# More pairs of column blocks by seven products in the MLP, with their sums of weights on GpSimd

## The chip, the cores and the metric

The kernel runs on one core of one Trainium2 chip. The metric is the device time of one execution, in microseconds (us). A core has TensorE (PE) for products of matrices, VectorE (DVE), ScalarE (ACT) and GpSimd (POOL) for elementwise work, and SyncE (SP), whose queue issues nearly all loads here. All arithmetic is float32; a product runs as three products of a high and a low part.

## The reference, cut to what matters

Two layers, each with a block of four mixers and an MLP. Only the MLP is touched by the change:

```python
h2 = _rms(x, norm2_g[layer])
x = x + jnp.square(jax.nn.relu(h2 @ mlp_w1[layer])) @ mlp_w2[layer]
```

`x` is 256 by 2048, `mlp_w1` 2048 by 8192, `mlp_w2` 8192 by 2048.

## The kernel before

**Blocks and chunks.** W1 is cut into 16 blocks of 512 columns, W2 into 16 blocks as well (four rounds `rd` of 2048 rows by four blocks `n` of 512 columns). Each block is loaded in eight chunks of 512 KB (256 rows, held as 128 partitions by 1024). A chunk becomes a high part `wh` (a copy by ACT, line 154) and a low part `wl` (raw minus high part by DVE, line 155). `raw` has four buffers, `wh` three, `wl` two. `product_steps` then issues twelve matmuls of 512 columns for a chunk: two halves of it, two tiles of 128 rows of the left side, three products each (lines 181, 182, 186).

**Pairs by seven products.** For a pair of blocks (b, b+1) the 2 by 2 product of half chunks with half tiles of rows (two row tiles, two halves of 256 rows of weights) is made of seven products in place of eight. `first` makes two of them (p1, p2) from the plain chunks of block b: six matmuls a chunk. Then, chunk by chunk, `sums_prep` loads the chunk of block b again into `b1` and that of block b+1 into `b2`, makes four sums of weights of 128 by 512 (`t13` holds two, `t24` two; lines 256, 257, 260, 261, each from two tiles in SBUF), and splits them and half of `b2` into high and low parts (`bh`, `bl`, `t13h`, `t13l`, `t24h`, `t24l`; lines 248 and 249). `sums_step` issues 15 matmuls with them (p3 to p7). After eight chunks `combine` adds p1 to p7 to the four results c11, c12, c21, c22 and squares their positive parts. `b1` and `b2` have one buffer each, `t13` and `t24` alternate in two buffers of one tag, `t24h` and `t24l` have one each; `t13h` and `t13l` take buffers from the rings of `wh` and `wl`.

The sum chain of one chunk: t13's halves are b2's first half minus b1's first half, and b2's second half minus b2's first half; t24's first half is b2's second half minus t13's first half, and t24's second half is t24's first half minus b1's second half. So line 260 is the last sum that reads `b2`, and line 261 the last that reads `b1`.

**What sets the order.** `mlp` runs a plan: plain W1 products (`plain`) and W2 products (`second`), chunk by chunk. Each chunk advances a clock by 2.72; whenever the clock passes `due`, the generator `steps` is advanced by a step of the pairs and yields how much is added to `due` (2.4 a chunk of `first`, 2.1 each of the five steps of a chunk of sums). The result is then placed on the engines by a list scheduler when the program is built, so that each engine has one fixed order. `place` transposes finished columns into the left side of a later W2 round (four `slots` groups). Of W1's sixteen blocks eight are plain and eight go as four pairs in each layer; the plan is four plain products, then three W2 rounds with two plain products behind the first and the second, then the fourth round.

## Time and profile before

| what | us |
|---|---|
| median of three runs | 2246.22 (2244.64 to 2248.01) |
| the profiled execution, its own time | 2246.25 |
| its span on the core | 2244.5 |
| PE busy in the span | 2216.0 (99%) |
| DVE busy | 1629.5 (73%) |
| ACT busy | 1196.8 (53%) |
| POOL busy | 148.0 (7%) |

Busy time is the time in which at least one instruction of the engine was running; a matmul's end is modelled, so neighbouring matmuls overlap and their distance from start to start says what one costs. The first MLP lies at some 431 to 1102 us of the span, the second at some 1545 to 2240. The time is 1.75 us more than the span. 444.29 MB move by DMA, 198 GB/s over the span.

### The profile page before, as it was taken

How to read it: one execution, taken by the hardware profiler on the slowest of the kernel's cores; microseconds unless marked ns; L12 is line 12 of the kernel's file. 1: busy time of each engine (PE TensorE's matmuls, PEld its weight loads, DVE VectorE, ACT ScalarE, POOL GpSimd, SP SyncE). 2: the span in 40 equal slices, each digit the busy share in tenths (PEclk: the TensorE clock that was granted, in tenths of full speed). 3: DMA queues.
4: the chain of work that ended last, by engine and by line, in shares of the span. 5: the costliest groups of instructions: out<-in, count | busy, mean ns of one | idle time of the engine just before them, and what ended most of it. 6: DMA issues, size and time to landing. Idle time of an engine off the chain costs nothing.

```text
span 2244.5 us, 30247 instructions
## 1 busy us (share of the span) xinstructions
PE 2216.0 (99%) x10988; PEld 1814.2 (81%) x10988; DVE 1629.5 (73%) x2421; ACT 1196.8 (53%) x1588; POOL 148.0 (7%) x402
## 2 busy tenths in 40 slices
PE   8999999999999999999999999999999999999999
PEld 7788788888788787888888877888887888888887
DVE  8877666877777778776578766658777776777754
ACT  6465444765555645645545554447555555465443
POOL 1221220100000000000011321101000000000000
PEclk9999999999999999999999999999999999999999
DMA  7536445566765666656556363456666666666554
GB/s 254 164 115 200 154 141 196 184 227 209 237 219 210 226 214 225 227 198 209 181 185 187 100 234 123 155 193 204 221 213 233 214 218 231 219 226 218 184 197 169
DMA packets 125429, 444.29 MB, mean 198 GB/s; under 512 B 15072, under 2 KB 15328, under 8 KB 125280
## 3 DMA queue, kind: packets, MB, share of 16 engines
q1 hardware_dynamic: 122688, 439.67, 58.0%
q10 hardware_dynamic: 2592, 2.70, 0.4%
q8 instruction: 86, 1.41, 0.3%
q14 instruction: 63, 0.52, 0.1%
HBM read 440.21 MB, written 2.10 MB: 197 GB/s over the span
## 4 chain that ended last, share of the span: by engine, by line
PE 91%; DVE 3%; DMA 2%; POOL 2%; issue 1%; ACT 1%; DVEq 0%; SPq 0%; ACTq 0%
PE mm L186 24%; PE mm L181 23%; PE mm L182 23%; PE p L223 4%; PE p L225 4%; PE p L224 4%; PE tp L312 2%; DMA raw<-in_w_dram 1%; DVE wl L155 1%; PE yp L713 1%; PE bu L693 1%; PE glu L736 1%; PE nsc L944 0%; PE npv L954 0%; ACT wh L154 0%
## 5 line engine op out<-in xcount | busy, mean ns | idle before, releaser
L154 ACT ACTIVATE wh<-raw 128x1024 fp32r<-128x1024 f32 (+1 forms) x688 | 716.0, 1049 | 763.5 <-PE mm L182 548.9
L155 DVE TENSOR_TENSOR wl<-raw,wh 128x1024 fp32r<-128x1024 f32 (+1 forms) x688 | 830.9, 1212 | 295.6 <-PE mm L186 187.0
L181 PE MATMUL mm<-wh,Bl 128*128 128x512 f32 x1280 | 500.0, 391 | 2.0 <-ACT wh L154 2.0
L182 PE MATMUL mm<-wh,Bh 128*128 128x512 f32 x1280 | 500.6, 391 | 0.0
L181 PE MATMUL mm<-wh,Al 128*128 128x512 f32 (+1 forms) x1216 | 471.0, 389 | 4.5 <-ACT wh L154 4.5
L182 PE MATMUL mm<-wh,Ah 128*128 128x512 f32 (+1 forms) x1216 | 471.2, 389 | 0.0
L186 PE MATMUL mm<-wl,Bh 128*128 128x512 f32 x1280 | 350.1, 393 | 2.5 <-DVE wl L155 2.4
L186 PE MATMUL mm<-wl,Ah 128*128 128x512 f32 (+1 forms) x1216 | 333.6, 394 | 9.4 <-DVE wl L155 9.2
L181 PEld LDWEIGHTS mm<-wh,Bl 128*128 128x128 f32 x1280 | 240.3, 188 | 54.6 <-ACT wh L154 3.7
L186 PEld LDWEIGHTS mm<-wl,Bh 128*128 128x128 f32 x1280 | 237.9, 188 | 55.5 <-DVE wl L155 5.9
L182 PEld LDWEIGHTS mm<-wh,Bh 128*128 128x128 f32 x1280 | 240.3, 188 | 50.7
L186 PEld LDWEIGHTS mm<-wl,Ah 128*128 128x128 f32 x1216 | 222.6, 189 | 64.0 <-DVE wl L155 14.7
L181 PEld LDWEIGHTS mm<-wh,Al 128*128 128x128 f32 x1216 | 229.8, 189 | 53.2 <-ACT wh L154 5.3
L182 PEld LDWEIGHTS mm<-wh,Ah 128*128 128x128 f32 x1216 | 229.7, 189 | 46.8 <-issue 1.1
L249 DVE TENSOR_TENSOR t13l<-t,t13h 128x1024 fp32r<-128x1024 f32 x64 | 78.4, 1224 | 88.7 <-PE mm L186 68.8
L248 ACT ACTIVATE t13h<-t 128x1024 fp32r<-128x1024 f32 x64 | 67.8, 1059 | 108.4 <-PE mm L182 93.8
L1121 DVE TENSOR_TENSOR x<-mm,x 128x512 f32<-128x512 f32 x96 | 62.1, 685 | 54.3 <-PE mm L186 54.1
L249 DVE TENSOR_TENSOR t24l<-t,t24h 128x1024 fp32r<-128x1024 f32 x64 | 78.1, 1220 | 4.5 <-ACT t24h L248 4.5
L248 ACT ACTIVATE t24h<-t 128x1024 fp32r<-128x1024 f32 x64 | 67.0, 1047 | 1.3 <-DVE t L261 0.7
L326 DVE TENSOR_TENSOR Bl<-tp,Bh 128x512 fp32r<-128x512 f32 x76 | 51.1, 685 | 12.6 <-ACT Bh L325 12.4
L248 ACT ACTIVATE bh<-b 128x512 fp32r<-128x512 f32 x64 | 40.1, 627 | 30.9 <-DMA b<-in_w_dram 30.9
L325 ACT ACTIVATE Bh<-tp 128x512 fp32r<-128x512 f32 x76 | 43.3, 588 | 21.4 <-PE tp L312 20.8
(399 smaller groups left out, 2346.7 us busy)
## 6 DMA issues: line engine op xcount, KB each, us to landing
raw<-in_w_dram SPq DMA_DIRECT2D x448, 512.0 KB, 4.2
raw<-in_w_main_dram SPq DMA_DIRECT2D x160, 512.0 KB, 3.7
b<-in_w_dram SPq DMA_DIRECT2D x128, 512.0 KB, 4.1
raw<-in_w_out_dram SPq DMA_DIRECT2D x64, 512.0 KB, 3.8
aux<-in_wcmp_dram SPq DMA_DIRECT2D x16, 512.0 KB, 5.8
raw<-in_w_gate_dram SPq DMA_DIRECT2D x16, 268.0 KB, 2.8
x<-in_x_dram SPq DMA_DIRECT2D x8, 256.0 KB, 4.7
aux<-in_s5g_dram SPq DMA_DIRECT2D x4, 512.0 KB, 6.0
```

The lines of the kernel that those rows point to most:

```text
L154: self.nc.scalar.activation(h[:, :cols], r[:, :cols], AF.Copy)
L155: self.nc.vector.tensor_tensor(l[:, :cols], r[:, :cols], h[:, :cols].bitcast(F32), ALU.subtract)
L181: nc.tensor.matmul(acc[t], rows(xl, t), mov(wh, j), start=k == 0, stop=False)
L182: nc.tensor.matmul(acc[t], rows(xh, t), mov(wh, j), start=False, stop=False)
L186: nc.tensor.matmul(acc[t], rows(lhs[k][0], t), mov(wl, j), start=False, stop=k == nk - 1)
L223: nc.tensor.matmul(acc, xl, wh, start=first, stop=False)
L224: nc.tensor.matmul(acc, xh, wh, start=False, stop=False)
L225: nc.tensor.matmul(acc, xh, wl, start=False, stop=last)
L248: nc.scalar.activation(h, x, AF.Copy)
L249: V.tensor_tensor(l, x, h.bitcast(F32), ALU.subtract)
L326: nc.vector.tensor_tensor(l, pt, h.bitcast(F32), ALU.subtract)
L1121: self.nc.vector.tensor_tensor(x, acc[t], x, ALU.add)
```

## The change

In each layer seven pairs in place of four: only blocks 0 and 1 stay plain. The four sums of weights of a chunk move from DVE to GpSimd (`G`). A chunk of `first` now adds 1.05 to `due`, each step of a chunk of sums 0.84, and `due` starts at zero, so that pair 0 lies beside the two plain products and two pairs lie beside each of the first three W2 rounds; the fourth round has none. `combine` reads the products in another order, and results go to other buffers (`late`). Line numbers behind 244 grow by one: what was 256, 257, 260, 261 is 257, 258, 261, 262.

```diff
--- before.py
+++ after.py
@@ -241,6 +241,7 @@
 
         nc = self.nc
         V = nc.vector
+        G = nc.gpsimd
         f2 = lambda x: x.rearrange("p a b -> p (a b)")
         ahead = lambda: self.tc.high_priority(offset=self.prio - 100)
 
@@ -253,12 +254,12 @@
             nc.sync.dma_start(f2(b1), src1)
             nc.sync.dma_start(f2(b2), src2)
             ta, tb = (self.wk.tile([P, 2, 512], F32, name=nm, tag="aux", bufs=2) for nm in ("t13", "t24"))
-            V.tensor_tensor(ta[:, 0, :], b2[:, 0, :], b1[:, 0, :], ALU.subtract)
-            V.tensor_tensor(ta[:, 1, :], b2[:, 1, :], b2[:, 0, :], ALU.subtract)
+            G.tensor_tensor(ta[:, 0, :], b2[:, 0, :], b1[:, 0, :], ALU.subtract)
+            G.tensor_tensor(ta[:, 1, :], b2[:, 1, :], b2[:, 0, :], ALU.subtract)
         yield
         with ahead():
-            V.tensor_tensor(tb[:, 0, :], b2[:, 1, :], ta[:, 0, :], ALU.subtract)
-            V.tensor_tensor(tb[:, 1, :], tb[:, 0, :], b1[:, 1, :], ALU.subtract)
+            G.tensor_tensor(tb[:, 0, :], b2[:, 1, :], ta[:, 0, :], ALU.subtract)
+            G.tensor_tensor(tb[:, 1, :], tb[:, 0, :], b1[:, 1, :], ALU.subtract)
         yield
         with ahead():
             bh = self.wk.tile([P, 512], F32R, name="bh", tag="z")
@@ -279,7 +280,7 @@
     def sums_step(self, acc, w, slot, sums, first, last):
 
         if first:
-            for i in (3, 5, 7, 6, 4):
+            for i in (6, 3, 5, 7, 4):
                 pool, tag = (self.ps, "mm") if i == 4 else (self.pm, "ms")
                 acc[i] = pool.tile([P, 512], F32, name=f"p{i}", tag=tag)
         for i, m in ((3, 3), (5, 0), (7, 2), (6, 1)):
@@ -1166,11 +1167,13 @@
                     self.act2(hs[t], acc[t], r, t)
             at(now[0] + 5, lambda: place(rd, n, hs))
 
+        late = lambda i: i and i % 2 == 0
+
         def first(i, b):
             p = []
             yield from self.first_steps(p, w1(b), h2)
             with self.hp():
-                v, c = tmp("v", ("rtmp", "sq")[i % 2]), tmp("c11", "rp" if i % 2 else "ev")
+                v, c = tmp("v", ("rtmp", "sq")[i % 2]), tmp("c11", "rp" if late(i) else "ev")
                 nc.scalar.activation(v, p[0], AF.Copy)
                 V.tensor_tensor(c, p[1], v, ALU.add)
                 self.act2(c, c, r, 0)
@@ -1179,19 +1182,21 @@
         def combine(i, p):
             v, c11 = firsts.pop(i)
             with self.hp():
-                tags = ("rp", "rp", "w") if i == 3 else ("ev", "ev", "ev")
+                tags = ("rp", "rp", "w") if late(i) else ("ev", "ev", "ev")
                 c12, c21, c22 = (tmp(nm, tag) for nm, tag in zip(("c12", "c21", "c22"), tags))
-                V.tensor_tensor(c12, p[3], v, ALU.add)
-                V.tensor_tensor(c12, p[5], c12, ALU.add)
-                V.tensor_tensor(c12, p[6], c12, ALU.add)
+                V.tensor_tensor(v, p[6], v, ALU.add)
+                V.tensor_tensor(c12, p[5], v, ALU.add)
+                V.tensor_tensor(c12, p[3], c12, ALU.add)
                 self.act2(c12, c12, r, 0)
-                V.tensor_tensor(v, p[6], v, ALU.add)
                 V.tensor_tensor(v, p[7], v, ALU.add)
+                V.tensor_tensor(c21, v, p[4], ALU.subtract)
+                self.act2(c21, c21, r, 1)
                 V.tensor_tensor(c22, p[5], v, ALU.add)
                 self.act2(c22, c22, r, 1)
-                V.tensor_tensor(c21, v, p[4], ALU.subtract)
-                self.act2(c21, c21, r, 1)
             ready[i] = (c11, c21), (c12, c22)
+            if i == 0:
+                at(now[0] + 5, lambda: place(0, 2, ready[0][0]))
+                at(now[0] + 8, lambda: place(0, 3, ready[0][1]))
 
         def second(rd, n, hooks={}):
             acc = []
@@ -1216,34 +1221,33 @@
                         self.sumsq(ss, n)
             yield
 
-        pairs = (4, 8, 12, 14)
+        pairs = (2, 4, 6, 8, 10, 12, 14)
 
         def steps():
...
             for i, b in enumerate(pairs):
                 for _ in first(i, b):
-                    yield 2.4
+                    yield 1.05
                 p = {}
                 for c in range(8):
                     w = []
                     for _ in self.sums_prep(w, w1(b)[c], w1(b + 1)[c]):
-                        yield 2.1
+                        yield 0.84
                     self.sums_step(p, w[0], h2[c], sums[c], c == 0, c == 7)
                     if c == 7:
                         combine(i, p)
-                    yield 2.1
-
-        plan = [plain(0, n) for n in range(4)]
+                    yield 0.84
+
+        plan = [plain(0, n) for n in range(2)]
         for rd in range(3):
-            put = {3: lambda rd=rd: place(rd + 1, 0, ready[rd][0]), 5: lambda rd=rd: place(rd + 1, 1, ready[rd][1])}
-            if rd == 2:
-                put[7] = lambda: place(3, 2, ready[3][0])
-            plan += [second(rd, n, put if n == 3 else {}) for n in range(4)]
-            if rd < 2:
-                plan += [plain(rd + 1, n) for n in (2, 3)]
-        plan += [second(3, n, {} if n else {1: lambda: place(3, 3, ready[3][1])}) for n in range(4)]
+            a, b = 2 * rd + 1, 2 * rd + 2
+            put = {3: lambda rd=rd, a=a: place(rd + 1, 0, ready[a][0]), 5: lambda rd=rd, a=a: place(rd + 1, 1, ready[a][1]),
+                   7: lambda rd=rd, b=b: place(rd + 1, 2, ready[b][0])}
+            rest = {1: lambda rd=rd, b=b: place(rd, 3, ready[b - 2][1])} if rd else {}
+            plan += [second(rd, n, {0: rest, 3: put}.get(n, {})) for n in range(4)]
+        plan += [second(3, n, {} if n else {1: lambda: place(3, 3, ready[6][1])}) for n in range(4)]
         ys = steps()
-        due = 5.0
+        due = 0.0
         for xs in plan:
             for _ in xs:
```

How the built program stands on the engines, at three places. Pairs and rounds are counted from 0. First GpSimd, beside W2's round 1, in pair 4: the rows of two neighbouring chunks of sums. Before, GpSimd has no row in the MLP outside of the norms; the sums of a chunk stand among DVE's rows, here those of a chunk of pair 1. Numbers behind a name tell buffers' uses apart.

```order
L249 TENSOR_TENSOR bl_6168<-b2_6118,bh_6167 128x512
L256 TENSOR_TENSOR t13_6121<-b2_6118,b1_6117 128x512
L257 TENSOR_TENSOR t13_6121<-b2_6118 128x512
L155 TENSOR_TENSOR wl_6039<-raw_6036,wh_6038 128x1024
L249 TENSOR_TENSOR t13l_6059<-t13_6012,t13h_6058 128x1024
L260 TENSOR_TENSOR t24_6122<-b2_6118,t13_6121 128x512
L261 TENSOR_TENSOR t24_6122<-t24_6122,b1_6117 128x512
L155 TENSOR_TENSOR wl_6065<-raw_6062,wh_6064 128x1024
L249 TENSOR_TENSOR t24l_6176<-t24_6122,t24h_6175 128x1024
```

In the changed kernel GpSimd has them, and nothing between:

```order
L258 TENSOR_TENSOR t13_7834<-b2_7831 128x512
L257 TENSOR_TENSOR t13_7834<-b2_7831,b1_7830 128x512
L261 TENSOR_TENSOR t24_7835<-b2_7831,t13_7834 128x512
L262 TENSOR_TENSOR t24_7835<-t24_7835,b1_7830 128x512
L258 TENSOR_TENSOR t13_7891<-b2_7888 128x512
L257 TENSOR_TENSOR t13_7891<-b2_7888,b1_7887 128x512
L261 TENSOR_TENSOR t24_7892<-b2_7888,t13_7891 128x512
L262 TENSOR_TENSOR t24_7892<-t24_7892,b1_7887 128x512
```

The four sums left DVE's queue, and the sum from `b2` alone now stands first. DVE keeps the splits; the same two chunks there in the changed kernel:

```order
L250 TENSOR_TENSOR bl_7841<-b2_7831,bh_7840 128x512
L155 TENSOR_TENSOR wl_7813<-raw_7810,wh_7812 128x1024
L250 TENSOR_TENSOR t13l_7845<-t13_7834,t13h_7844 128x1024
L1122 TENSOR_TENSOR x0_78<-mm0_7493,x0_78 128x512
L1122 TENSOR_TENSOR x1_79<-mm1_7494,x1_79 128x512
L155 TENSOR_TENSOR wl_7857<-raw_7854,wh_7856 128x1024
L250 TENSOR_TENSOR t24l_7849<-t24_7835,t24h_7848 128x1024
L250 TENSOR_TENSOR bl_7916<-b2_7888,bh_7915 128x512
L155 TENSOR_TENSOR wl_7900<-raw_7897,wh_7899 128x1024
L250 TENSOR_TENSOR t13l_7920<-t13_7891,t13h_7919 128x1024
```

There is one split of a W2 chunk (`wl`) for each group of three splits of the sums or a little more, and it stands right behind `t13l` or between `bl` and `t13l`. Second, SP's queue at the same place in the changed kernel, where `b2` and `b1` are loaded for chunk after chunk, with the W2 chunks (`raw`) between:

```order
L141 DMA raw_7942<-in_w2_dram 128x1024
L255 DMA b2_7831<-in_w1_dram 128x1024
L254 DMA b1_7830<-in_w1_dram 128x1024
L141 DMA raw_7978<-in_w2_dram 128x1024
L255 DMA b2_7888<-in_w1_dram 128x1024
L254 DMA b1_7887<-in_w1_dram 128x1024
L141 DMA raw_8043<-in_w2_dram 128x1024
```

Before, some four loads of `raw` stand between two pairs of `b2` and `b1`; now it is one or two. Third, DVE where pair 4 ends and pair 5 begins: `t24l_8374` and `bl_8330` belong to the first chunk of sums of pair 5, `wl_8168` to the second chunk that `first` takes from its block.

```order
L155 TENSOR_TENSOR wl_8156<-raw_8153,wh_8155 128x1024
L1189 TENSOR_TENSOR c12_8088<-p3_7608,c12_8088 128x512
L1191 TENSOR_TENSOR v_7543<-p7_7610,v_7543 128x512
L250 TENSOR_TENSOR t24l_8374<-t24_8324,t24h_8373 128x1024
L1192 TENSOR_TENSOR c21_8089<-v_7543,p4_7611 128x512
L1194 TENSOR_TENSOR c22_8090<-p5_7609,v_7543 128x512
L250 TENSOR_TENSOR bl_8330<-b2_8320,bh_8329 128x512
L155 TENSOR_TENSOR wl_8168<-raw_8165,wh_8167 128x1024
```

Such a place before (pair 1 ends), where the first sums of the next pair already stand in DVE's own queue:

```order
L257 TENSOR_TENSOR t13_7217<-b2_7214 128x512
L155 TENSOR_TENSOR wl_6824<-raw_6821,wh_6823 128x1024
L256 TENSOR_TENSOR t13_7217<-b2_7214,b1_7213 128x512
L155 TENSOR_TENSOR wl_6844<-raw_6841,wh_6843 128x1024
L1186 TENSOR_TENSOR c12_6805<-p6_5973,c12_6805 128x512
L1188 TENSOR_TENSOR v_5884<-p6_5973,v_5884 128x512
L155 TENSOR_TENSOR wl_6850<-raw_6847,wh_6849 128x1024
L1189 TENSOR_TENSOR v_5884<-p7_5972,v_5884 128x512
L155 TENSOR_TENSOR wl_6874<-raw_6871,wh_6873 128x1024
```

At the change of pairs a split of a sum that GpSimd makes now stands ahead of splits of plain chunks.

## Rows read from the trace of the kernel before

**Rows 1.** The page, part 1: engine, busy us (share of the span) xinstructions.

```profile
PE 2216.0 (99%) x10988; PEld 1814.2 (81%) x10988; DVE 1629.5 (73%) x2421; ACT 1196.8 (53%) x1588; POOL 148.0 (7%) x402
```

**Rows 2.** The page, part 4: the chain of waits that ended last, share by engine.

```profile
PE 91%; DVE 3%; DMA 2%; POOL 2%; issue 1%; ACT 1%; DVEq 0%; SPq 0%; ACTq 0%
```

**Rows 3.** Windows: length, busy us (xinstructions) of PE, PEld, DVE, ACT, POOL; clock, DMA share, GB/s.

```profile
412.00:1115.00 703.00, 698.89 (x3121) 570.84 (x3120) 517.79 (x598) 389.50 (x471) 8.74 (x17) 1.00 0.62 214
1530.00:2244.50 714.50, 709.59 (x3160) 579.48 (x3158) 513.07 (x571) 379.75 (x444) 7.15 (x14) 1.00 0.62 213
```

**Rows 4.** Timeline of PE, first layer's W_out: start us, duration us, engine, line, operation.

```profile
409.50 0.39 PE L181 MATMUL mm<-wh,Bl 128*128 128x512 f32 x1
...
412.89 0.39 PE L182 MATMUL mm<-wh,Bh 128*128 128x512 f32 x1
```

**Rows 5.** Groups of DVE by line, 412 to 1115 us: xcount | busy us, mean ns | idle.

```profile
L155 DVE TENSOR_TENSOR wl<-raw,wh 128x1024 fp32r<-128x1024 f32 x223 | 271.3, 1222 | 99.6 <-PE mm L186 50.0 <-PE p L225 23.3 <-issue 15.4
L249 DVE TENSOR_TENSOR t13l<-t,t13h 128x1024 fp32r<-128x1024 f32 x32 | 39.2, 1224 | 44.1 <-PE mm L186 34.6 <-issue 7.4 <-ACT wh L154 2.2
...
L256 DVE TENSOR_TENSOR t<-b,b 128x512 f32<-128x512 f32 x31 | 21.3, 686 | 2.0 <-DMA b<-in_w_dram 1.8
```

**Rows 6.** Timeline of DVE in the second layer's mixers, 1283 to 1289 us.

```profile
1283.11 1.22 DVE L155 TENSOR_TENSOR wl<-raw,wh 128x1024 fp32r<-128x1024 f32 x1
1284.24 0.69 DVE L677 TENSOR_TENSOR sc<-w,cs 128x512 f32<-128x512 f32 x1
1284.84 0.69 DVE L678 TENSOR_TENSOR ss<-w,cs 128x512 f32<-128x512 f32 x1
...
1286.11 2.36 DVE L155 TENSOR_TENSOR wl<-raw,wh 128x1024 fp32r<-128x1024 f32 x2
1288.38 0.74 DVE L675 TENSOR_TENSOR_SCAN w<-mag,z 128x128 f32<-128x128 f32 x2
```

**Rows 7.** Timeline of POOL over the same stretch.

```profile
1283.28 5.58 POOL L87 TENSOR_SCALAR hv<-hv 128x8 f32<-128x8 f32 x1 [10.62 <-DVE hv L521]
```

**Rows 8.** Timeline of POOL, 263 to 264.2 us.

```profile
263.41 0.64 POOL L748 TENSOR_SCALAR_AFFINE_SELECT np<-np 128x512 f32<-128x512 f32 x1 [1.76 <-ACT np L946]
```

**Rows 9.** Timeline of DVE, 263 to 267 us.

```profile
263.50 1.62 DVE L155 TENSOR_TENSOR wl<-raw,wh 128x1024 fp32r<-128x1024 f32 x1 [0.23 <-PE mm L186]
...
266.28 1.23 DVE L155 TENSOR_TENSOR wl<-raw,wh 128x1024 fp32r<-128x1024 f32 x1 [0.48 <-issue]
```

**Rows 10.** Groups of POOL, 1268.7 to 1272.3 us, DVE not in the way.

```profile
L93 POOL TENSOR_TENSOR drs<-drs,rst 128x4 f32<-128x4 f32 x3 | 0.6, 199 | 0.2
```

**Rows 11.** Groups of POOL, 1217.2 to 1220 us.

```profile
L93 POOL TENSOR_TENSOR hc<-hc,rst 128x16 f32<-128x16 f32 x3 | 0.7, 222 | 0.2
```

**Rows 12.** Groups of POOL, 1256 to 1262 us.

```profile
L748 POOL TENSOR_SCALAR_AFFINE_SELECT dp<-dp 128x512 f32<-128x512 f32 x2 | 1.3, 634 | 0.0
```

**Rows 13.** The load of `b2` (line 254): its landing.

```profile
DMA to landing us min/median/max: 3.1/3.2/5.5
```

**Rows 14.** The load of `b1` (line 253): its landing.

```profile
DMA to landing us min/median/max: 3.2/4.7/6.4
```

**Rows 15.** Waits of SP's queue: us in total, times, longest us.

```profile
SPq L254 <- DVE t L260: 201.7, 60, 4.8
```

**Rows 16.** Timeline of DVE, 630 to 636 us: the last two sums of one chunk.

```profile
633.92 0.69 DVE L260 TENSOR_TENSOR t<-b,t 128x512 f32<-128x512 f32 x1
```

**Rows 17.** Timeline of SP, 634 to 636 us: the next loads of `b2` and `b1`.

```profile
634.68 0.33 SPq L254 DMA_DIRECT2D b<-in_w_dram  x1
635.37 0.33 SPq L253 DMA_DIRECT2D b<-in_w_dram  x1
```

**Rows 18.** Windows of ten us with the highest DMA rates, of the span and of the MLP.

```profile
10.00:20.00 10.00, 10.00 (x44) 8.29 (x43) 10.00 (x36) 9.59 (x21) 0.00 (x0) 1.00 1.00 359
...
1010.00:1020.00 10.00, 10.00 (x47) 8.15 (x46) 7.88 (x12) 5.21 (x8) 0.00 (x0) 1.00 0.86 295
```

**Rows 19.** The page, part 5: ACT's high part of `t13`, xcount | busy us, mean ns | idle.

```profile
L248 ACT ACTIVATE t13h<-t 128x1024 fp32r<-128x1024 f32 x64 | 67.8, 1059 | 108.4 <-PE mm L182 93.8
```

## The prediction

> **What bounds the kernel now.** I read the page's parts on engines and on the chain of waits first: PE is busy 99% of the span and holds 91% of the chain [rows 1, 2]. So the end is set by how many matmuls PE has to do and by nothing else for long. Then the windows over the two MLPs: PE is idle for 4.1 us of 703 in the first and 4.9 us of 714.5 in the second, while DVE is busy some 73%, ACT some 55% and GpSimd 1% [rows 3]. The clock granted there is 1.00, its upper level of 2.4 GHz. The reader is to see two things: a matmul taken away is time won as long as the others keep up, and there is no reserve in PE's few idle microseconds, so each new wait of PE is paid in full. Then the timelines of DVE and GpSimd side by side, at the places where both are at work. These decide the forecast, since the change puts 448 sums on GpSimd in the stretch where DVE is busiest.
>
> **What the change takes from PE.** A plain pair of blocks costs 192 matmuls (two blocks, eight chunks, twelve), one by seven products 168 (eight chunks, 6 and 15). Three more pairs in each of two layers: 144 matmuls less. From 409.50 to 412.89 us are 15 steps from start to start, 0.226 us each [rows 4]. So 144 x 0.226 = **32.5 us** off, if PE never waits. The profiled execution has its own time of 2246.25 us, 1.75 over its span and practically the median of the runs (2246.22); the sum is made against it. All MLP work but the fourth W2 round gets denser: two pairs beside each of three rounds.
>
> **What a sum costs on GpSimd.** The trace shows no sum of 128x512 there. An addition or product of two tiles takes 199 ns at 128x4 and 222 ns at 128x16 [rows 10, 11], 1.92 ns an element, which gives 0.199 + 508 x 0.00192 = 1.17 us at 512. The bounds: 0.63 us, a 128x512 instruction with one input [rows 12], and twice that, 1.27. I take 1.17, as it comes from instructions with two inputs; with the 0.07 us idle that those show between dependent ones, 1.25 from start to start. On DVE a sum takes 0.69 and a new one starts every 0.60 [rows 5, 6].
>
> **GpSimd and DVE block each other.** At 1283.28 us GpSimd starts an instruction on 128x8 that takes 5.58 us [rows 7]. Over that time DVE runs splits and sums with two tiles of SBUF as inputs, one directly behind another, until 1288.38; GpSimd ends at 1288.86, 0.5 us later [rows 6]. The other way round: at 263.41 GpSimd has an instruction of 0.64 us, and the split that DVE starts at 263.50 takes 1.62 us instead of 1.23 [rows 8, 9]; the port is free 0.16 us before GpSimd's end. So a GpSimd instruction and a DVE instruction with two SBUF inputs run one after the other. All splits of weights are of that kind. The Trainium skill, "SBUF — State Buffer", section "Who interferes with whom", speaks against this change in that sense: a DVE instruction with two SBUF inputs contends with a GpSimd instruction that reads SBUF. Its further rule, that who issues first gets the port for the whole instruction, is not what these rows show (a waiting GpSimd instruction was passed by six of DVE's); it is weighed as a rival below.
>
> **The chain of a chunk of sums.** `b1` has one buffer. So the next load of `b1` starts when GpSimd has ended line 262, and the next chunk's lines 257, 261 and 262 follow that landing. Today the sums on DVE make the same ring, and SP waits for line 260 sixty times, 4.8 us at most [rows 15], but a chunk of sums has some 14 us of PE's work beside it in its order. In the new order PE has some 237 matmuls' worth between the first use of `t13h` in chunk 0 and that in chunk 7: 53.6 us, 7.66 a chunk. The ring costs:
> - three sums, 3 x 1.25 = 3.75 us (2.1 to 4.05 by the bounds above);
> - from the sum's end to the issue 0.1 us (633.92 + 0.69 to 634.68 for `b2` today [rows 16, 17]);
> - landing 3.2 to 4.7 us: the median of `b2`, issued alone, and that of `b1`, issued 0.7 us behind `b2` [rows 13, 14]. The new `b1` is issued a sum or more behind `b2`, but with a W2 chunk behind it: I take 3.95, the middle;
> - blocking. `t13h` is ready 1.06 us after line 257 [rows 19], before line 261 ends, so DVE's `t13l` takes the port ahead of line 262: 1.13 us [rows 6]. In about a third of the chunks a W2 split follows directly in DVE's order and goes ahead too: another 0.38 on average. Together 1.5 (0 to 3.4: nothing, or `t13l`, a W2 split and another one ahead of line 257).
>
> The sum is 9.3 us a chunk, with bounds of 6.5 and 12.2. Chunk 1 can't start ahead: its sums go into the buffer of `t13`, which is free when `t13l` of chunk 0 is made (1.2 us), then two sums (2.5) and `t13h` (1.2): 4.9 us. So `t13h` of chunk 7 is there 4.9 + 6 x 9.3 = 60.7 us after that of chunk 0; PE wants it after 53.6. **PE waits 7.1 us in each of 14 pairs: 99 us.** A cross-check by the port alone: a chunk of sums needs 2 x 1.13 + 0.60 for its splits, 1.5 x 1.13 for W2's, and 4 x (1.17 - 0.16) for the sums, 8.6 us of 7.66. Even packed without a gap that is 6.6 us a pair too much.
>
> **The change of pairs.** DVE is in order, and `t24l` of the next pair's first chunk now stands ahead of the splits of plain chunks. After line 262 of chunk 7: load 4.05, three sums 3.75, blocking 1.1, `t24h` and `t24l` 2.3, then two additions of `combine`, `bl` and the first `wl` behind (2.9): 14.1 us. PE until then has `t24h` to wait for (1.1) and 41 matmuls (9.3): 10.4. It waits 3.7 us at the place that I counted; at the others the order differs, so I take 3 (0 to 5) for twelve changes: **36 us**. SP's queue is in order as well, and loads of plain chunks stand behind `b2` and `b1`; four `raw` buffers cover that.
>
> **What is hidden.** DVE loses 256 sums and gets 48 more chunks of three splits, 48 fewer `wl` and six more `combine`; it stays below its present load, and these sit beside PE's work. ACT's work on them is covered likewise (55% busy today). Each new pair loads its first block twice, 48 loads of 0.52 MB more; on average 469 MB in the span. The other reading order of `combine` and the other buffers cost nothing that I can price: all that PE waits for in both MLPs today is 9 us [rows 3].
>
> **The sum.** 2246.25 - 32.5 + 99 + 36 = **2349 us**, slower by 4.6%.
>
> **Rivals.**
> - *The ring fits, faster.* If the landing is 3.2 us and only `t13l` blocks, a chunk takes 3.75 + 0.1 + 3.2 + 1.13 = 8.2, the wait is 0.5 us a pair (7 us), and 12 to 24 at the changes: 2233 to 2245. If blocking costs nothing and the changes neither, 2214. For it: the loads then have more room than today. Against: the port's 8.6 us of 7.66. It decides below 8.1 us a chunk (53.6 less 4.9, by six). 0.13.
> - *A little over.* A chunk of 8.3 to 8.7 us with changes of 1 to 2 us: 2241 to 2287. 0.13.
> - *One passes, not six.* If a waiting GpSimd instruction gets the port at the next end of a DVE instruction, blocking is 1.13 and a chunk 8.9: 4.9 us a pair, 69 in all, 2319. This is inside the forecast's own range. The Trainium skill's rule on issue order, same page and section, would make this the case.
> - *Starved sums, slower still.* If DVE's splits pass as in the 5.58 us above at each chunk, blocking is 3.4, a chunk 11.2: 18.5 us a pair, with 5 at the changes 2533. For it: a PE that waits leaves DVE with ready splits. Against: DVE itself waits for the sums and then frees the port. 0.12.
> - *Loads decide between pairs.* There PE has 28 us for some 17 loads of 0.52 MB, 326 GB/s; ten us of today's MLP reach 295, the span's best 359 [rows 18]. At 295 it is 31 us, the same 3 us that stand in the sum with another releaser, so the time would be 2349 too.
>
> **How the numbers follow.** The forecast, 2290 to 2440 (a chunk of 8.7 to 10.2 us), has 0.62 with the loads' case. The rest is as given: 0.13, 0.13, 0.12. The measurement tells 0.2%, 4.5 us, from no change. Faster by that: the first rival's 0.13 and a little of the second's, 0.14; the same 0.04; slower 0.82. The range of 2232 to 2450 leaves out the better half of the first rival and most of the starved case, 0.08 and 0.10.
>
> **What the profile after would show.** Matmuls: 144 fewer. GpSimd: 448 instructions on lines 257 to 262 whose mean, waits for the port in it, lies over 1.17 us, at 1.5 or so, line 262's highest; under 0.9 would make the size of the sums wrong. DVE's `wl` mean above today's 1222 ns [rows 5]. SP's loads of `b1` 9 us apart inside a pair; 7.7 would be the first rival. PE idle some 140 us more in the MLPs, ended by ACT's `t13h` and `bh` inside the pairs and by DVE's `wl` and `bl` at the changes. If PE's idle time is as small as today, the prediction is wrong at the ring; if it is large but ended by loads of `raw`, at the change of pairs.

## The result, and the profile after

The changed kernel takes 2452.41 us, the median of four runs (2445.97 to 2455.69), where the kernel before took 2246.59 us beside it: a ratio of 1.0913 with an interval of 1.0889 to 1.0937. The forecast was 2349 us with a range of 2232 to 2450. The sign and the kind of cause were right. The size was half of what came: 103 us forecast, 206 measured, and the time lies 2 us above the range. The profiled execution has a span of 2451.7 us and its own time of 2453.45, again 1.75 more.

The page of the changed kernel, parts 1 and 4 (the columns of [rows 1, 2]):

```profile
PE 2280.1 (93%) x10844; PEld 1796.0 (73%) x10844; DVE 1871.2 (76%) x2295; ACT 1273.1 (52%) x1692; POOL 943.3 (38%) x850
...
PE 49%; POOL 19%; DMA 13%; DVE 10%; issue 5%; ACT 3%; SPq 0%; DVEq 0%; POOLq 0%; ACTq 0%
```

PE has 144 matmuls fewer, as meant. Its share of the chain falls from 91% to 49%, and GpSimd, which had 2%, now holds 19%. DVE has 126 instructions fewer than in [rows 1] and is busy 242 us longer: as the timelines below show, time in which an instruction waits for its turn counts as busy.

Windows over the two MLPs of the changed kernel (columns of [rows 3]):

```profile
431.00:1212.00 781.00, 709.36 (x2953) 542.11 (x2953) 623.45 (x510) 411.19 (x498) 406.56 (x237) 0.98 0.60 204
1640.00:2451.00 811.00, 734.48 (x3047) 566.26 (x3045) 626.67 (x499) 410.29 (x482) 399.00 (x234) 0.97 0.59 201
```

PE is idle for 71.6 and 76.5 us, 148 in all, where it was idle for 9. What it waits for, in the list of PE's waits (us in total, times, longest):

```profile
PE mm L186 <- DVE wl L155: 72.6, 61, 4.9
PE p L223 <- ACT t13h L249: 27.2, 19, 2.5
PE mm L181 <- ACT wh L154: 9.8, 12, 2.0
PE p L225 <- DVE wl L155: 9.4, 9, 2.7
PE p L225 <- DVE bl L250: 9.3, 20, 0.6
```

The first row is the one to notice. PE waits most for `wl`, DVE's split of plain and of W2 chunks, which has nothing to do with the sums. `t13h`, at the end of the sums' own chain, comes second. The list leaves some lost time unnamed: a wait shorter than some 0.16 us (0.39 of a matmul's duration less 0.23 from start to start) disappears in a matmul's modelled end.

The groups of DVE and GpSimd that matter, from part 5 of the same page (xcount | busy us, mean ns | idle):

```profile
L155 DVE TENSOR_TENSOR wl<-raw,wh 128x1024 fp32r<-128x1024 f32 (+1 forms) x640 | 915.6, 1440 | 189.1 <-PE mm L186 128.0
...
L261 POOL TENSOR_TENSOR t<-b,t 128x512 f32<-128x512 f32 x112 | 189.3, 1690 | 233.3 <-DVE t13l L250 210.5
...
L258 POOL TENSOR_TENSOR t<-b 128x512 f32<-128x512 f32 x112 | 187.0, 1670 | 210.7 <-DMA b<-in_w_dram 138.9
L250 DVE TENSOR_TENSOR t13l<-t,t13h 128x1024 fp32r<-128x1024 f32 x112 | 188.0, 1678 | 88.6 <-ACT t13h L249 70.0
...
L262 POOL TENSOR_TENSOR t<-t,b 128x512 f32<-128x512 f32 x112 | 235.0, 2098 | 8.6
L257 POOL TENSOR_TENSOR t<-b,b 128x512 f32<-128x512 f32 x112 | 184.1, 1644 | 128.9 <-DMA b<-in_w_dram 109.2
```

Both sides are stretched. `wl` takes 1440 ns on average over the whole program, where the page of the kernel before has 1212 (both with a few short ones in them), and `t13l` 1678, where [rows 5] had 1224. The sums take 1644 to 2098 ns, with a least time of line 262 of 1275 ns. First `wl` before, then line 262 of the changed kernel (least, median and longest time in ns):

```profile
L155 DVE TENSOR_TENSOR wl<-raw,wh 128x1024 fp32r<-128x1024 f32 (+1 forms) x688 | 830.9, 1212 | 295.6 <-PE mm L186 187.0
...
L262 POOL TENSOR_TENSOR t<-t,b x112: 1275/2152/2254, 337.0 to 2342.0; 128x512 f32<-128x512 f32 x112
```

How that comes about is seen where a pair ends. The timelines of GpSimd and of DVE of the changed kernel over the same stretch (start, duration, then what the engine waited for before it):

```profile
1838.29 1.44 POOL L257 TENSOR_TENSOR t<-b,b 128x512 f32<-128x512 f32 x1 [0.27 <-DMA b<-in_w_dram]
1839.80 2.13 POOL L261 TENSOR_TENSOR t<-b,t 128x512 f32<-128x512 f32 x1
1842.00 2.15 POOL L262 TENSOR_TENSOR t<-t,b 128x512 f32<-128x512 f32 x1
```

```profile
1838.49 4.52 DVE L155 TENSOR_TENSOR wl<-raw,wh 128x1024 fp32r<-128x1024 f32 x2
1842.93 0.68 DVE L1187 TENSOR_TENSOR v<-p,v 128x512 f32<-128x512 f32 x1
```

Two splits that take 1.22 us each [rows 5] fill 4.52 us, since a sum goes first each time: sum, split, sum, split, sum. Each sum but the first takes 2.1 us instead of 1.27, and each split 2.3 instead of 1.2. This is not the picture of [rows 6, 7], where a waiting GpSimd instruction was passed by six of DVE's. Here, with work queued on both sides, they take turns.

The pace of a pair, from the starts of ACT's `t13h` in the timeline (here chunks 1 to 4 of pair 0):

```profile
461.23 1.06 ACT L249 ACTIVATE t13h<-t 128x1024 fp32r<-128x1024 f32 x1 [0.58 <-DVE wl L155]
469.64 1.06 ACT L249 ACTIVATE t13h<-t 128x1024 fp32r<-128x1024 f32 x1 [4.93 <-POOL t L257]
478.42 1.06 ACT L249 ACTIVATE t13h<-t 128x1024 fp32r<-128x1024 f32 x1 [3.60 <-POOL t L257]
489.32 1.06 ACT L249 ACTIVATE t13h<-t 128x1024 fp32r<-128x1024 f32 x1 [3.23 <-POOL t L257]
```

Over the 14 pairs, the time from the `t13h` of chunk 0 to that of chunk 7 is 63.4 to 70.6 us, 65.9 on average: 6.5 from chunk 0 to 1, and 9.9 a chunk from there. From chunk 7 to the next pair's chunk 0 it is 33.3 to 37.8 us, 35.4 on average.

PE takes up a `t13h` somewhat after it is made, later for chunk 0 than for chunk 7, so its own times are the ones to hold against its work. PE's first use of `t13h` in chunk 0 and in chunk 7 of pair 0, and in chunk 0 of pair 1:

```profile
453.60 0.40 PE L223 MATMUL p<-t13h,Sl 128*128 128x512 f32 x1
...
520.48 0.39 PE L223 MATMUL p<-t13h,Sl 128*128 128x512 f32 x1
...
558.25 0.40 PE L223 MATMUL p<-t13h,Sl 128*128 128x512 f32 x1
```

These are 66.9 and 37.8 us; on average over all pairs and changes it is 64.7 us from chunk 0 to chunk 7 and 37.2 from there to the next pair.

### The profile page after: what moved, and what is told of

Its sections match the earlier page's. It is cut to its first block, busy times and chain, and to the rows that moved or that the text cites. A ratio compares the mean times of both kernels' runs of the same rounds, so it can differ in the third digit from the quotient of the medians.

```text
span 2451.7 us, 30847 instructions
## 1 busy us (share of the span) xinstructions
PE 2280.1 (93%) x10844; PEld 1796.0 (73%) x10844; DVE 1871.2 (76%) x2295; ACT 1273.1 (52%) x1692; POOL 943.3 (38%) x850
## 4 chain that ended last, share of the span: by engine, by line
PE 49%; POOL 19%; DMA 13%; DVE 10%; issue 5%; ACT 3%; SPq 0%; DVEq 0%; POOLq 0%; ACTq 0%
PE mm L181 12%; PE mm L182 12%; PE mm L186 12%; DMA b<-in_w_dram 11%; POOL t L257 5%; POOL t L261 5%; DVE wl L155 5%; POOL t L258 4%; POOL t L262 3%; PE p L223 2%; PE p L225 2%; PE p L224 2%; DMA raw<-in_w_dram 2%; ACT wh L154 1%; PE tp L313 1%
## 5 line engine op out<-in xcount | busy, mean ns | idle before, releaser
L155 DVE TENSOR_TENSOR wl<-raw,wh 128x1024 fp32r<-128x1024 f32 (+1 forms) x640 | 915.6, 1440 | 189.1 <-PE mm L186 128.0
L181 PE MATMUL mm<-wh,Al 128*128 128x512 f32 (+1 forms) x832 | 322.5, 390 | 4.5 <-DVE scr L124 4.2
L182 PE MATMUL mm<-wh,Ah 128*128 128x512 f32 (+1 forms) x832 | 322.3, 390 | 0.0
L261 POOL TENSOR_TENSOR t<-b,t 128x512 f32<-128x512 f32 x112 | 189.3, 1690 | 233.3 <-DVE t13l L250 210.5
L258 POOL TENSOR_TENSOR t<-b 128x512 f32<-128x512 f32 x112 | 187.0, 1670 | 210.7 <-DMA b<-in_w_dram 138.9
L250 DVE TENSOR_TENSOR t13l<-t,t13h 128x1024 fp32r<-128x1024 f32 x112 | 188.0, 1678 | 88.6 <-ACT t13h L249 70.0
L186 PE MATMUL mm<-wl,Ah 128*128 128x512 f32 (+1 forms) x832 | 227.7, 394 | 15.7 <-DVE wl L155 15.6
L262 POOL TENSOR_TENSOR t<-t,b 128x512 f32<-128x512 f32 x112 | 235.0, 2098 | 8.6
L257 POOL TENSOR_TENSOR t<-b,b 128x512 f32<-128x512 f32 x112 | 184.1, 1644 | 128.9 <-DMA b<-in_w_dram 109.2
L250 DVE TENSOR_TENSOR t24l<-t,t24h 128x1024 fp32r<-128x1024 f32 x112 | 159.5, 1424 | 92.0 <-ACT t24h L249 81.3
```

The costliest lines, as they stand in the source:

```text
L155: self.nc.vector.tensor_tensor(l[:, :cols], r[:, :cols], h[:, :cols].bitcast(F32), ALU.subtract)
L181: nc.tensor.matmul(acc[t], rows(xl, t), mov(wh, j), start=k == 0, stop=False)
L182: nc.tensor.matmul(acc[t], rows(xh, t), mov(wh, j), start=False, stop=False)
L186: nc.tensor.matmul(acc[t], rows(lhs[k][0], t), mov(wl, j), start=False, stop=k == nk - 1)
L250: V.tensor_tensor(l, x, h.bitcast(F32), ALU.subtract)
L257: G.tensor_tensor(ta[:, 0, :], b2[:, 0, :], b1[:, 0, :], ALU.subtract)
```

## Experiments

Eleven kernels were run. The question of the first seven was what holds the changed kernel: the sums' arithmetic, the port that they share with DVE, or the loads of `b1` and `b2`, which have one buffer each. The last four ask what is left of the loss without either, whether the change's smaller parts cost anything, and whether fewer pairs would win. Each ratio is against the kernel before in the same comparison. Where a kernel has one run, no interval is given.

**1. The sums back on DVE.** The changed kernel with all else in the source as it is (the scheduler orders the rows anew):

```diff
-            G.tensor_tensor(ta[:, 0, :], b2[:, 0, :], b1[:, 0, :], ALU.subtract)
+            V.tensor_tensor(ta[:, 0, :], b2[:, 0, :], b1[:, 0, :], ALU.subtract)
...
```

(and so for the other three).

> The changed kernel with its four sums of weights on DVE again, all else as it is (the planner orders the rows anew). Theory, the ring through GpSimd: a sum then costs 0.6 us in place of 1.26 and waits for no port, three of them 2 to 3 us in place of 5.7 with one or two splits between; a chunk's ring falls from 9.9 to 7.4 to 8.0 us against 7.66 of PE's work, so most of the 205 us go: 2215 to 2280. Rival, the single buffers and their loads (4.3 us to land) with two pairs a round are too dense wherever the sums are made: over 2380.

Measured: 2314.67 us (2312.11 to 2319.26), ratio 1.0298 (1.0282 to 1.0315). Both missed. GpSimd is to blame for 138 of the 206 us, but seven pairs also lose with the sums on DVE, 101 us over the 2213.7 that the count of matmuls gives. The span from the `t13h` of chunk 0 to that of chunk 7 is 58.9 us a pair on average, of 53.6 of PE's work.

**2. The kernel before, with its sums on GpSimd.** Four pairs, and the same four lines changed the other way.

> The kernel before, four pairs a layer, with its four sums of weights on GpSimd. The ring is then about 10 us a chunk against some 14 us of PE's work, so it fits. Theory: within 10 us of the kernel before (2236 to 2257), although 256 sums contend for the port. Rival, the port itself (each sum holds up DVE's splits and PE with them, wherever it stands): 256 of 448 sums, so 100 us or more over, 2340 and up.

Measured: 2255.34 us (2253.77 to 2257.44), ratio 1.0030 (1.0018 to 1.0043). The theory holds: 256 sums on GpSimd cost 7.5 us where a chunk of sums has 14 us of other work around it. The same instruction on the same engine costs 138 us in all when 448 of them stand close. Its `wl` takes 1334 ns on average there, more than the 1212 on the page of the kernel before, and PE hardly notices:

```profile
L155 DVE TENSOR_TENSOR wl<-raw,wh 128x1024 fp32r<-128x1024 f32 (+1 forms) x688 | 913.0, 1334 | 355.6 <-PE mm L186 263.6 <-PE p L225 50.4 <-issue 14.9
```

**3. No reload.** The changed kernel, with `b1` and `b2` loaded for a pair's first chunk alone:

```diff
-            nc.sync.dma_start(f2(b1), src1)
-            nc.sync.dma_start(f2(b2), src2)
+            if load:
+                nc.sync.dma_start(f2(self.bb[0]), src1)
+                nc.sync.dma_start(f2(self.bb[1]), src2)
...
-                    for _ in self.sums_prep(w, w1(b)[c], w1(b + 1)[c]):
+                    for _ in self.sums_prep(w, w1(b)[c], w1(b + 1)[c], c == 0):
```

> The changed kernel where b1 and b2 are loaded for the first chunk of each pair alone and used for all eight (the other loads are left out). The ring then holds no load; sums and splits are as many as before, on the same engines. Theory: ring and port both count; without the load the port's 8.6 to 9.0 us a chunk are left of 9.9, a pair has 55 to 58 us where it had 66, and the changes of pairs get 2 us shorter: 2300 to 2350. Rival, the load in the ring is all: a chunk falls to PE's 7.7 us, 2215 to 2270. Rival, the port is all: 9.9 us stays, over 2400.

Measured: 2429.32 us (one run). The forecast's ring of a load behind a sum is gone, and only 23 us with it. The third answer, that the port alone is enough, is the one whose time came, though not with its 9.9 us a chunk: a chunk takes 9.0 us here from `t13h` to `t13h`. At the changes of pairs PE loses 8.3 us each over its own work, nearly what it loses in the changed kernel (8.7, below). GpSimd's and DVE's timelines of this kernel show the turns without a gap:

```profile
574.67 1.30 POOL L259 TENSOR_TENSOR t<-b,b 128x512 f32<-128x512 f32 x1
575.92 2.30 POOL L260 TENSOR_TENSOR t<-b 128x512 f32<-128x512 f32 x1
578.17 2.28 POOL L263 TENSOR_TENSOR t<-b,t 128x512 f32<-128x512 f32 x1
580.53 2.16 POOL L264 TENSOR_TENSOR t<-t,b 128x512 f32<-128x512 f32 x1
582.65 1.27 POOL L259 TENSOR_TENSOR t<-b,b 128x512 f32<-128x512 f32 x1
```

```profile
575.84 1.23 DVE L250 TENSOR_TENSOR t24l<-t,t24h 128x1024 fp32r<-128x1024 f32 x1 [2.28 <-ACT t24h L249]
576.98 2.32 DVE L155 TENSOR_TENSOR wl<-raw,wh 128x1024 fp32r<-128x1024 f32 x1
579.34 2.19 DVE L250 TENSOR_TENSOR t13l<-t,t13h 128x1024 fp32r<-128x1024 f32 x1
```

Four sums take 8.0 us (574.67 to 582.65) with three splits between them, and GpSimd is never idle in this stretch. The 7.66 us that PE has for a chunk are gone before any load is counted.

**4. No sums.** The changed kernel, with `t13` and `t24` split straight from `b1` and `b2`:

```diff
-            ta, tb = (self.wk.tile([P, 2, 512], F32, name=nm, tag="aux", bufs=2) for nm in ("t13", "t24"))
-            G.tensor_tensor(ta[:, 0, :], b2[:, 0, :], b1[:, 0, :], ALU.subtract)
+            ta, tb = b1, b2
...
```

> The changed kernel without the four sums of weights: t13 and t24 are split from b1 and b2 themselves (the sums are left out, all loads, splits and matmuls stay). Theory: the ring is then load 4.3 us, high part 1.06, low part 1.13 and waits, 6.5 to 7.5 us a chunk, less than PE's work: 2214 to 2240, the 32.5 us of the matmuls off. Rival, the 25 MB more of loads or the denser splits decide: over 2300.

Measured: 2271.0 us (one run), between the two answers. Without any sum the reloads still cost 57 us over 2214. The next load waits for the buffers, which are held here until their splits are done; in the list of the waits of SP's queue (us in total, times, longest) the load of `b2` stands with

```profile
SPq L255 <- DVE t24l L250: 226.8, 104, 3.8
```

**5. Fills in place of sums.** Experiment 3, with each sum replaced by two fills of the same 128 by 512, so that GpSimd works nearly as long (two fills take 1.05 us, a sum 1.26 at least) but reads nothing:

```diff
-            G.tensor_tensor(ta[:, 0, :], b2[:, 0, :], b1[:, 0, :], ALU.subtract)
+            G.memset(ta[:, 0, :], 0.5)
+            G.memset(ta[:, 0, :], 0.5)
...
```

> As e3 (b1 and b2 loaded once a pair), with each of the four sums on GpSimd replaced by two fills of the same 128x512 half with a constant: the sums are left out, GpSimd only writes. Two fills take some 1.1 us together (one is 0.52 us in the trace of before), near a sum's 1.26, and stand in the same chain with the splits. Theory, the read port shared with DVE: without a read no split waits, the means of wl and t13l come back to 1.22 us, and most of e3's 182 us over the kernel before go: 2220 to 2270. Rival, GpSimd's own time and the chain of GpSimd, ACT and DVE decide, port or not: over 2370.

Measured: 2221.28 us (two runs, 2220.68 and 2221.87), ratio 0.9886 (0.9867 to 0.9906). This is the decisive pair. Against experiment 3 the reading is gone, with it each sum's wait for its inputs and 0.2 us of its length. The shorter work is 94 us of GpSimd's time at most (0.21 for each of 448), and the kernel's time falls by 208 us. The groups of DVE's split in experiment 3, and of the split and a fill here:

```profile
L155 DVE TENSOR_TENSOR wl<-raw,wh 128x1024 fp32r<-128x1024 f32 x624 | 913.6, 1473 | 198.2 <-PE mm L186 146.3 <-PE p L225 18.8 <-issue 11.5
```

```profile
L155 DVE TENSOR_TENSOR wl<-raw,wh 128x1024 fp32r<-128x1024 f32 x624 | 760.5, 1224 | 321.3 <-PE mm L186 199.5 <-PE p L225 83.3 <-issue 15.9
...
L262 POOL MEMSET t<- 128x512 f32 x112 | 59.0, 527 | 0.0
```

`wl` is back at the 1.22 us of [rows 5] beside 896 fills of 0.53 us. The Trainium skill, "SBUF — State Buffer", section "Who interferes with whom", says that a DVE instruction with two SBUF inputs contends with a GpSimd instruction that reads SBUF and not with one that only writes it. Here the trace agrees on both halves, 1473 ns against 1224.

**6. No sums and no reload.** Experiments 3 and 4 together.

> As e4 (no sums: t13 and t24 split from b1 and b2), and b1 and b2 loaded once a pair as in e3, so 103 MB of loads less. e4 took 2271, 57 us over the 2214 of the matmuls alone. Theory, those 57 us are waits for loads, the ring of b1 and b2 among them: 2214 to 2230. Rival, they are DVE's order and its denser splits: 2255 to 2275.

Measured: 2211.17 us (two runs, 2210.46 and 2211.89), ratio 0.9841 (0.9822 to 0.9861). This is where the count of matmuls, 2246.25 - 32.5 = 2213.7, said that the end would be. So without the sums and the reloads nothing of the changed kernel's loss is left.

**7. Half of the sums.** `t13`'s two sums on DVE, `t24`'s two on GpSimd:

```diff
-            G.tensor_tensor(ta[:, 0, :], b2[:, 0, :], b1[:, 0, :], ALU.subtract)
-            G.tensor_tensor(ta[:, 1, :], b2[:, 1, :], b2[:, 0, :], ALU.subtract)
+            V.tensor_tensor(ta[:, 0, :], b2[:, 0, :], b1[:, 0, :], ALU.subtract)
+            V.tensor_tensor(ta[:, 1, :], b2[:, 1, :], b2[:, 0, :], ALU.subtract)
```

> The changed kernel with two of its four sums (those of t13) on DVE and two (those of t24) on GpSimd. Theory, port and queue of DVE and GpSimd are one resource, a sum costing it 1.1 us on GpSimd and 0.6 on DVE: halfway between e1 (2315) and the changed kernel (2452), 2360 to 2400. Rival, the chain of four sums on GpSimd in front of the next load decides, and shortening it by two frees PE: under 2330.

Measured: 2355.35 us (2353.09 to 2357.17), ratio 1.0480 (1.0462 to 1.0497), 5 us under the theory's range and far from the rival's. Halving GpSimd's sums takes away 97 of the 138 us between the two ends: of the three shares that were run, all on DVE is best.

**8. Sums on DVE and no reload.** Experiments 1 and 3 together.

> The changed kernel with the four sums on DVE and with b1 and b2 loaded for the first chunk of a pair alone (the later chunks sum the same weights again, so the loads are left out). Theory: with the sums on DVE nothing holds the port against it, and per chunk DVE has some 7.0 us of 7.66 (2 x 1.13 + 0.60 of splits, 1.5 x 1.13 for W2, 4 x 0.60 of sums); so what the first experiment lost (2315) was the ring of loads, and without it the time is 2215 to 2250. Rival: the sums crowd DVE itself at 80% busy, so the time stays above 2275 though nothing is loaded again.

Measured: 2266.98 us (2264.59 to 2267.53), ratio 1.0087 (1.0071 to 1.0104): between the answers. The ring of loads takes 48 of the 101 us of experiment 1, and 53 stay with the sums on a DVE that is busy 81% of the span. The trace shows where these lie. From first use to first use, as above, and less the time of its own matmuls, PE loses 11 us in all inside the 14 pairs, as much as in experiment 6; at the 12 changes of pairs it loses 62, where experiment 6 has 10. Its longest item in the list of waits is `combine`'s first addition, once for each change:

```profile
PE p L223 <- DVE v L1189: 22.3, 12, 3.5
```

With these, the six combinations are complete:

| time, us | no sums | sums on DVE | sums on GpSimd |
|---|---|---|---|
| `b1`, `b2` loaded once a pair | 2211 | 2267 | 2429 |
| loaded for each chunk | 2271 | 2315 | 2452 |

Along a row the sums cost 44 to 56 us on DVE and 181 to 218 on GpSimd. Down a column the reloads cost 60, 48 and 23: the more the sums hold the kernel up, the less the loads add.

**9. The two smaller parts alone.** The kernel before with the products in the order 6, 3, 5, 7, 4 and the new order of `combine`:

```diff
-            for i in (3, 5, 7, 6, 4):
+            for i in (6, 3, 5, 7, 4):
...
```

> The kernel before with the change's two smaller parts alone: products taken up in the order 6, 3, 5, 7, 4 and the new order of combine. Theory: these cost nothing, 2241 to 2252. Rival: they hold banks of PSUM or DVE longer and carry part of the loss: over 2257.

Measured: 2249.32 us (2247.53 to 2251.27), ratio 1.0009 (1.0000 to 1.0018). At most 4 us, more likely 2: the forecast's nothing.

**10 and 11. Five pairs.** If density is what costs, one pair more might win. In the kernel before blocks 10 and 11 become a pair; three pairs are spread about as before and the last two packed, with the sums on DVE (10) and on GpSimd (11):

```diff
-        pairs = (4, 8, 12, 14)
+        pairs = (4, 8, 10, 12, 14)
+        rate = (84, 84, 108, 52, 52)
...
-                    yield 2.4
+                    yield rate[i] / 40
...
-                        yield 2.1
+                        yield rate[i] / 50
```

> The kernel before with five pairs a layer in place of four: blocks 10 and 11 go as a pair too, sums on DVE as before. Three pairs keep a chunk of sums every 8.4 to 10.8 of the plan's clock, the last two are packed to 5.2 (before 10.5, in the changed kernel 4.2). 48 matmuls fewer, 48 x 0.226 = 10.8 us. Theory: what costs time is how densely the sums stand, and the ring with sums on DVE takes some 8.4 us a chunk, about what PE has there (38 matmuls, 8.7 us), so most of the gain stays: 2234 to 2248. Rival: the dense pairs lose what they lost with seven pairs and the sums on DVE (2315 - 2214 = 101 us over 14 pairs, 7.2 each), four times: 2250 to 2265.

> The same five pairs with their four sums a chunk on GpSimd. Theory of the shared port and density: the six spread pairs cost what 256 sums cost before (about 1 us a pair), the four packed ones have a ring of 9.9 us of 8.7, some 7 us a pair and 3 at their changes: 2262 to 2285. Rival: the sums' number decides and not their density; then 320 of 448 sums cost 320/448 of the 238 us that the changed kernel lost against its count of matmuls, 170 us: about 2405.

Measured: 2255.38 us on DVE (2252.79 to 2259.48), ratio 1.0030 (1.0019 to 1.0042), and 2310.61 us on GpSimd (2307.99 to 2320.53), ratio 1.0277 (1.0250 to 1.0304). In 10 the rival came true: 2238 by the count, so the packed pairs lose more than the 10.8 us that the fifth pair brings. In 11 neither range holds it, and the trace says where the loss lies. Windows of kernel 11 over the first MLP; the `t13h` of the three spread pairs run until 831 us, those of the two packed ones from 871 on:

```profile
431.00:580.00 149.00, 147.11 (x660) 119.68 (x659) 111.89 (x104) 91.69 (x119) 62.66 (x48) 1.00 0.66 223
580.00:800.00 220.00, 215.84 (x948) 175.81 (x947) 152.80 (x130) 117.56 (x132) 79.81 (x50) 0.99 0.66 217
800.00:950.00 150.00, 143.47 (x622) 114.02 (x622) 115.50 (x98) 78.19 (x90) 73.96 (x41) 0.99 0.62 213
950.00:1150.00 200.00, 186.80 (x805) 147.64 (x804) 140.63 (x142) 103.99 (x132) 57.71 (x35) 0.97 0.59 196
```

PE is idle for 6 us in the first 369 and for 20 in the last 350. Between kernels 10 and 11, the `t13h` of chunk 7 of the last pair moves by 24 us in the first layer (1025.7 to 1050.0): 5 of these come before the first of the packed pairs, 19 in these two. So the place where the sums stand close decides, as the theory has it, but its range was too low: 19 us for two packed pairs is about the 7 and 3 us that I gave each of them, while the 17 us that experiment 10 loses against its count, with the sums on DVE, were left out. No version that was run beats the kernel before with all of its computation.

## Why the prediction was half right

**The matmuls: right.** 10988 to 10844, and experiment 6 ends at 2211.17 where 2213.7 was worked out.

**The size of a sum: at its upper bound.** I took 1.17 us from small instructions with two inputs; the least times are 1.26 to 1.28, the bound of 1.27 that came from doubling the one-input instruction [rows 12].

**The ring inside a pair: right in kind, too short.** The steps, forecast and measured:

| step | forecast, us | measured, us |
|---|---|---|
| three sums with their blocking | 3.75 + 1.5 = 5.25 | 1.64 + 1.69 + 2.10 and two gaps of 0.07, 5.6 |
| landing of `b1` | 3.95 | 4.3 |
| a chunk | 9.3 | 9.9 |
| chunk 0 to chunk 1 | 4.9 | 6.5 |
| chunk 0 to chunk 7 | 60.7 | 65.9 |
| for PE, from first use to first use | 60.7 | 64.7 |
| over PE's 53.6, 14 times | 99 | 155 |

The landing of `b1` in the changed kernel, beside [rows 14]:

```profile
DMA to landing us min/median/max: 3.1/4.3/5.8
```

A miss of 0.6 us a chunk and of 1.6 at the start makes 5.2 us a pair between the `t13h`. PE gets back 1.2 of them, as it takes up the first `t13h` that much later, and waits 11.1 us in place of 7.1: 56 us more in 14 pairs. That is the leverage of such a sum: PE's 7.66 us are fixed, so only the excess counts, and some 6% on the chunk raise the excess by more than half.

**The step that failed: who is held up.** Under "blocking" I delayed only GpSimd's sums by DVE's splits. A sum delays a split as well. PE waits directly for `wl` and `bl`, and I costed that at nothing ("it stays below its present load, and these sit beside PE's work"). In the trace PE waits for `wl` 82 us on its two lines, 33 of them inside pairs and 33 at their changes (by the starts of `t13h`), and in experiment 3, with no ring of loads, 2429 us are left. My cross-check by the port alone stood beside the ring and gave 8.6 us a chunk; it was the second limit and should have been priced for itself. The ring's terms add up to the pace of the changed kernel, but the port alone gives 218 of its 241 us over 2211. Removing either one does not give back what the other holds.

**The change of pairs: too low by a factor of three.** 36 us forecast, 3 for each of twelve. Measured are 37.2 us a change for 28.5 of PE's work: 8.7 us each, 104 in all. The same hole is in this term, since its splits stand in it at their full speed and only the sums have a "blocking". The kernel before loses 1.3 us in each of its 8 pairs and 1.75 at each of its 6 changes in the same count, 21 in all, which are in its time already. The sum is then -32.5 + 155 + 104 - 21 = 206, and 206 was measured.

**The sign that came true by luck.** PE was to be idle "some 140 us more in the MLPs", and it is: 148 against 9. But that was to be the whole loss. The loss is 238 us (206 + 32.5), and the profile's idle time holds only 139 of them; the rest would have to lie in waits too short to be seen and in matmuls that ran slower (below); how much each holds was not measured.

**The rivals.** The mechanism of "one passes, not six" is what the trace shows inside the MLP. The Trainium skill's rule on issue order ("SBUF — State Buffer", section "Who interferes with whom": who issues first, not the kind of instruction, decides who is blocked) agrees with the turns of 2.1 to 2.3 us; the 5.58 us of [rows 7] remain an exception. The price of 2319 that I worked out for it had the same hole as the forecast, as it made only the sums wait. "Starved sums" (2533) did not occur: no sum takes over 2.4 us. "Loads decide between pairs" is not borne out: loads of `raw` hold 2% of the chain of waits of the changed kernel, those of `b1` and `b2` 11% (part 4 of the page, by line). "The ring fits" fell with 9.9 us for 8.1, "a little over" with 9.9 for at most 8.7. Two slips in the working moved neither forecast nor range: with no blocking at all, as its bound says, the shortest chunk is 5.4 us and not 6.5, and 17 loads in 28 us are 318 GB/s and not 326.

**The clock: not foreseen.** Windows of 2 us of the changed kernel behind the second layer's second pair, and PE's timeline there (the columns of the windows are those of [rows 3]):

```profile
1842.00:1844.00 2.00, 0.94 (x4) 0.81 (x5) 1.77 (x3) 0.00 (x0) 2.00 (x1) 1.00 0.88 289
1844.00:1846.00 2.00, 2.00 (x7) 1.25 (x5) 1.84 (x3) 1.81 (x2) 0.15 (x1) 0.56 0.89 322
...
1850.00:1852.00 2.00, 2.00 (x6) 1.61 (x5) 2.00 (x3) 0.77 (x2) 1.03 (x1) 0.50 0.71 262
1852.00:1854.00 2.00, 2.00 (x6) 1.52 (x6) 2.00 (x4) 2.00 (x4) 0.00 (x0) 0.50 0.00 0
1854.00:1856.00 2.00, 2.00 (x10) 1.61 (x9) 1.05 (x1) 2.00 (x4) 0.00 (x0) 0.88 0.50 162
```

```profile
1843.06 1.20 PE L186 MATMUL mm<-wl,Bh 128*128 128x512 f32 x4 [3.00 <-DVE wl L155]
...
1848.98 0.79 PE L225 MATMUL p<-wl,Ah 128*128 128x512 f32 x1 [2.68 <-DVE wl L155]
1849.57 0.63 PE L223 MATMUL p<-wh,Al 128*128 128x512 f32 x1
1850.00 0.63 PE L224 MATMUL p<-wh,Ah 128*128 128x512 f32 x1
1850.42 0.63 PE L223 MATMUL p<-wh,Al 128*128 128x512 f32 x1
```

Both waits end with a `wl` that a sum had held up: the two of 4.52 us above, and one from 1847.02 on that took 1.91 us. After the first the granted clock falls from 1.00 to 0.50, the lower level of 1.2 GHz, and it is back at 1.00 by 1856. In between, matmuls start 0.43 us apart instead of the 0.226 of [rows 4]. Over the span the mean granted clock is 0.978, before 0.998. At a level of one half that is 2 x 0.022 x 2451.7 = 108 us at the lower level, before 9. By this estimate at most 50 us of PE's time (half of the 99 more) went that way, some of it inside waits that were there anyway; it is part of the times above, not on top of them. How much it cost by itself was not tried.

**Open.** A second buffer for `b1` and `b2`, which would loosen the ring and keep the computation, was not tried. Experiments 3 and 8, which leave nearly all of these loads out, suggest that it would give back some 23 us with the sums on GpSimd and 48 on DVE, not enough to win in either case.

## What to carry to other kernels

GpSimd is no free engine for sums of two SBUF tiles beside a DVE that reads two SBUF tiles: cost both engines' queues as one, with GpSimd's instructions at their full length, and ask which of DVE's instructions something waits for directly. Such an offload was nearly free here where the work stands far apart (7.5 us for 256 sums) and cost 138 us more than leaving the work on DVE where it stands close (448 sums). And where a forecast is an excess over a fixed time, two limits that each exceed it have to be priced separately, and a few per cent on one of them can raise the answer by half.

## What the runs showed of the hardware that I had not expected

- GpSimd and DVE took turns, one instruction each, when both had a queue of instructions with two SBUF inputs (2.3 us a split, 2.1 to 2.3 us a sum; in all of experiment 3 no sum takes over 2.38 us and no split over 2.37, so none waited for more than one of the other's), although in the kernel before one GpSimd instruction waited 5.58 us behind six of DVE's [rows 6, 7]. What tells the cases apart was not found.
- GpSimd's fills were untouched by DVE's two-input instructions and left them alone: 0.51 to 0.54 us for 128x512 in experiment 5, `wl` at 1.22 us on average.
- TensorE's granted clock fell to its lower level inside an MLP in which PE is busy 91% (734 of 811 us), after one wait of 3.00 us, with a second of 2.68 us while it was down, and was back some 10 us after it fell, behind 5 us of matmuls without a gap.
